# Where plain up parts end and block products begin: a four-layer hybrid trunk with one more plain part, later adaLN steps and another eviction

## The chip, the cores and the metric

The kernel runs on 1 core of a Trainium2 chip. The metric is device time in microseconds (us) of one execution; the median of several runs counts. The engines are TensorE (PE in the profile; PEld is its weight load), VectorE (DVE), ScalarE (ACT), GpSimd (POOL) and SyncE (SP, which only issues transfers here).

## The reference

The reference is two residual layers on x of shape (1024 tokens, 1024 channels) in float32, conditioned by a vector c. Each layer has a mixer and a channel mixer (FFN):

```python
for i in range(DEPTH):                         # DEPTH = 2
    mod = (silu(c) @ ada_w[i] + ada_b[i])      # adaLN: 6 x 1024 numbers
    sh_m, sc_m, g_m, sh_f, sc_f, g_f = split(mod, 6)
    hm = rms_norm(x, norm_mix[i]) * (1 + sc_m) + sh_m
    x = x + g_m * (even_mixer(hm) if i % 2 == 0 else odd_mixer(hm))
    hf = rms_norm(x, norm_ffn[i]) * (1 + sc_f) + sh_f
    x = x + g_f * conv_ffn(hf)

def conv_ffn(h, w_up, conv_w, conv_b, w_down):  # w_up 1024 x 5632, w_down 2816 x 1024
    gate, val = split(h @ w_up, 2)
    gate = causal_dwconv(gate, conv_w) + conv_b # width 3
    return (silu(gate) * val) @ w_down
```

The even mixer is gated linear attention in parallel with trailing-window pooling. The odd mixer is attention in three groups of 8 heads (dilations 1, 4 and 16 of the window); the groups' outputs are merged per head with weights from their softmax denominators, and an output projection of 1024 x 1024 follows:

```python
wts = softmax(stack(lses), axis=0)
o = sum(wts[..., None] * stack(outs), axis=0)
return o.reshape(B, T, 1024) @ w_out
```

## The kernel before, in words

Channels lie on the 128 partitions and tokens along the free dimension: x is 8 tiles of 128 x 1024, and every stage handles the tokens in two halves of 512 columns. Each float32 operand of a large product is split into a rounded high part and the rest (`split`, L185 on ACT and L186 on POOL or DVE), and one product of 128 x 128 by 128 x 512 becomes three matmuls: high x high, high x low, low x high (`mm3`, L212 to L214; L1392 to L1394 in the attention projections).

The kernel is written with a framework that plans the order on every engine when it is built: instructions that come earlier in the source have priority, and one whose inputs or buffers are not free yet, by the planner's own estimates of durations, is passed over for a later one. The order so planned is fixed. At run time each engine works through its own list and waits where an operand or a buffer is not there. `tc.issue_after(ins)` puts what is issued in its block behind `ins` on its engine.

The source's own order is made by generators. `weave(chain, dense)` runs a latency-bound chain of steps and, at each number that the chain yields, takes as much of a dense generator (one step is three matmuls) as that number of microseconds; `None` from the dense side means that it has nothing to give.

PSUM has two tiles of two banks (`mm_ps`, names `mm`) and four of one bank (`s_ps`, names `sp`). Buffers in SBUF that matter here: 24 of 128 x 1024 (`big`), 4 of raw weights (`raw`), 9 pairs of split weights (`whi`, `wlo`), 8 of 128 x 512 (`t2k`).

**The FFN's up projection** (`ffn`). It has 22 tiles (j), each of a gate and a value output of 128 channels. `first_two` computes tiles 0 and 1 directly: eight row blocks for each output and half, 96 `mm3` matmuls a tile. It starts on token half 0 while half 1 is still being normalised, and its last chain is the value output of tile 1, half 1, in an `mm_ps` tile that `act` (L1167) reads. The other tiles are formed from block products (`up`): 2 x 2 blocks of the weights and of h, seven products of 12 matmuls in place of eight, and sums before and after them. `h_sums` forms the sums of h once a layer (L1210, in place on the normalised x, then splits into `ext`, `t4` and the second half of h's own tiles), `w_sums(j)` those of the weights (L1265, four DVE additions, loads `wr` or, for the first such tile, `raw`), and `plus` (L1282) those of the products, which also frees their PSUM. In the source `w_sums(j + 1)` stands before `up(j)`. `conv` and `act` finish a tile (L1146, L1142, L1165, L1167) and store it to DRAM (`hid`).

The call of these steps before:

```python
sums = first_two()
a = w_sums(2)
if l == 0:
    secs_due[0], pace[0] = 24, 9
    with tc.issue_after(last_act[0].ins):
        step_back(True)
        step_back(True)
b = sums()
for j in range(2, NJ):
    nxt = w_sums(j + 1) if j < NJ - 1 else None
```

**adaLN.** The 24 sections of modulation columns are summed in the background. `step_back` is called with every group of three matmuls of the FFN and, once in `pace` calls, takes one step of `ada_steps`: a load of 256 KB into `raw` (L274, on SP) and one multiply-add, on DVE (L288, L290) while `by_pool` is false, on ACT and POOL (L284, L286) in the down projection, where `pace` is 2. A section takes ten steps; at the first FFN 14 sections are left.

**Attention** (`odd`). `dense` runs 12 projections of queries and keys and 6 of values; each qk part ends with a norm on ACT and DVE (L1403 to L1410) and, ten dense steps later, with the transposes on PE (L1424). `chains` runs 12 attention parts (`attend`), each of 24 steps. `merge(hp, need)` loads the three groups' outputs of one head pair (`ld`, three buffers, L1624, on SP), forms the weights on DVE and ACT (L1626 to L1634), sums (L1639 on ACT, L1641 on DVE) and transposes (L1647); it has eight load steps that yield `need` and four transposing ones that yield half of it. Two merges stand in the source after the attention parts 5 and 6, two more at the end, where `dense` has come to the output projection.

**The output projection** adds gate x (w_out rows x merged heads) to x, two row blocks at a time for head pairs 0 and 1 (`update` with `wide`), then four for pairs 2 and 3. With `wide="apart"` each 128 x 512 half of an `mm_ps` tile is scaled by ACT (L250) into a `t2k` tile and added by POOL (L251). With `wide=True`, which the even layer uses, one DVE instruction of 128 x 1024 (L253) does both when both halves are there.

Of the kernel before, what the change touches and what calls it, by code (L numbers as in the profile page):

```python
# [13 lines left out]
ALU = mybir.AluOpType  # L14
# [20 lines left out]
def trunk(ctx, tc, x, c, ada_w, ada_b, norm_mix, norm_ffn, ev_w_in, ev_w_out, gdn_conv_w,  # L35
# [35 lines left out]
    def t2k():  # L71
        return tmp("t2k", [P, HALF], 8)
# [153 lines left out]
    def update(rows, hid, gate, xt, order, wide=False, done=None):  # L226
# [7 lines left out]
        for o, hf in order:  # L234
# [10 lines left out]
            if not wide:  # L245
                nc.vector.scalar_tensor_tensor(out=xt[o][:, s], in0=p, scalar=gate[:, o:o + 1], in1=xt[o][:, s],  # L246
                                               op0=ALU.mult, op1=ALU.add)
            elif wide == "apart":
                t = t2k()
                nc.scalar.activation(t, p, AF.Copy, scale=gate[:, o:o + 1])  # L250
                nc.gpsimd.tensor_tensor(out=xt[o][:, s], in0=xt[o][:, s], in1=t, op=ALU.add)  # L251
            elif hf:
                nc.vector.scalar_tensor_tensor(out=xt[o], in0=ps, scalar=gate[:, o:o + 1], in1=xt[o],  # L253
                                               op0=ALU.mult, op1=ALU.add)
# [876 lines left out]
    def ffn(l, xt, h, vec, acc, vec_next):  # L1131
        gate = mod[l][:, 40:48]
        wu, wd = ffn_w_up[l], ffn_w_down[l]
        with tc.tile_pool(name=f"pf{l}", bufs=1) as pf:
# [25 lines left out]

            last_act = [None]

            def act(t, vps, j):

                nc.scalar.activation(t, t, AF.Silu)  # L1165
                for hf in range(2):
                    last_act[0] = nc.vector.tensor_tensor(out=t[:, HS[hf]], in0=t[:, HS[hf]], in1=vps[hf], op=ALU.mult)  # L1167
                nc.sync.dma_start(hid_d[l][j], t)
# [34 lines left out]
            KH = KT // 2  # L1203

            def h_sums():

# [30 lines left out]
            def w_sums(j):  # L1237

                raw = []
                for c0 in (j * P, DFF + j * P):  # L1240
                    if j == 2:
                        for q in range(2):
# [27 lines left out]
            def up(j, b, a):  # L1270
# [24 lines left out]
                act(t, (u, v), j)  # L1295

            sums = first_two()
            a = w_sums(2)
            if l == 0:
                secs_due[0], pace[0] = 24, 9  # L1300
                with tc.issue_after(last_act[0].ins):
                    step_back(True)
                    step_back(True)
            b = sums()
            for j in range(2, NJ):
                nxt = w_sums(j + 1) if j < NJ - 1 else None
# [21 lines left out]
    def odd(xt, h, vec, acc):  # L1328
# [5 lines left out]
        with tc.tile_pool(name="po", bufs=1) as po:  # L1334
# [130 lines left out]
            def dense():  # L1465
# [43 lines left out]
                for ks in ((0, 1), (2, 3)):  # L1509
                    upd = update(row_blocks(od_w_out[0], ks), o, gate, res["x"], BY_TILE, wide="apart")  # L1510
                    for n, c in enumerate(upd):
# [158 lines left out]
            def chains():  # L1670
                last = len(todo) - 1
                for i in range(last):
                    yield lambda: (i, 0) in ready
                    yield from attend(i, 1.7)
                    if i in (5, 6):
                        yield from merge(i - 5, 2.0)
                other = merge(2, 0)
# [91 lines left out]
```

## Time and profile before

| | |
|---|---|
| median of 3 runs | 3075.42 us (3072.78 to 3076.55) |
| the profiled execution | 3068.5 us, span 3066.5 us |
| PE busy | 2961.2 us, 97% of the span, 14362 matmuls |
| DVE busy | 1946.5 us, 63% |
| ACT, POOL busy | 1148.7 us (37%), 1056.6 us (34%) |
| granted PE clock, mean | 0.989 |
| DMA | 331.46 MB, 108 GB/s over the span |

A busy PE is an overlapped pipeline: a matmul of 512 columns is shown as about 0.39 us but the next starts 0.226 us later, so counts and start times tell more than busy shares. A line of the timeline has start, duration (both us), engine, source line, operation, what it writes and reads, how many alike were joined, and in brackets the idle time before it with what ended it. The stages of the span: the even mixer to about 545 us, the first FFN to about 1245, attention to about 2390, the second FFN to the end.

### The profile page before, as it was taken

The numbers are of one execution on the slowest core, as the hardware profiler recorded it, in microseconds if no ns is written. First come the engines' busy times: TensorE is split into PE (matmuls) and PEld (weight loads), VectorE is DVE, ScalarE is ACT, GpSimd is POOL, SyncE is SP. The second block draws the span as 40 slices with busy tenths as digits, with TensorE's granted clock in tenths as the row PEclk, the third lists the DMA queues.
The fourth block names the chain that finished last, engine by engine and source line by source line (L and its number), as shares of the span: only waits on it lengthen the run. The fifth ranks groups of instructions, "written<-read, shape, count | busy, mean of one in ns | idle before, by whom it ended". The sixth has DMA issues, their size and how long they took to land.

```text
span 3066.5 us, 40355 instructions
## 1 busy us (share of the span) xinstructions
PE 2961.2 (97%) x14362; PEld 2439.3 (80%) x14362; DVE 1946.5 (63%) x3770; ACT 1148.7 (37%) x2285; POOL 1056.6 (34%) x807
## 2 busy tenths in 40 slices
PE   7999999999999999999999999999988899999999
PEld 4777777778888888788888878888866688888888
DVE  6768735998886555554545546463667877766554
ACT  5434422533334433434243323333354433334210
POOL 3322223555556865200000000000064555556540
PEclk9999999999999999999999999999999999999999
DMA  7313323253333654413233242322243222224321
GB/s 257 107 46 99 89 80 133 76 182 113 110 118 133 211 156 139 145 35 102 62 95 89 80 127 77 108 71 94 72 169 106 81 84 83 83 83 168 110 91 58
DMA packets 274754, 331.46 MB, mean 108 GB/s; under 512 B 27155, under 2 KB 194170, under 8 KB 274554
## 3 DMA queue, kind: packets, MB, share of 16 engines
q1 hardware_dynamic: 266554, 300.54, 31.2%
q0 software_dynamic: 7040, 25.17, 2.4%
q10 hardware_dynamic: 960, 3.18, 0.3%
q8 instruction: 113, 1.85, 0.2%
q14 instruction: 87, 0.71, 0.1%
HBM read 251.82 MB, written 77.00 MB: 107 GB/s over the span
## 4 chain that ended last, share of the span: by engine, by line
PE 67%; DVE 8%; POOL 3%; DMA 3%; issue 3%; ACT 1%; SPq 0%; POOLq 0%; ACTq 0%; DVEq 0%
PE sp L212 9%; PE sp L214 9%; PE sp L213 9%; PE mm L1394 8%; PE mm L1392 8%; PE mm L1393 8%; PE mm L212 3%; PE mm L213 3%; PE mm L214 3%; PE sp L1588 2%; PE sp L1544 2%; PE sp L1424 1%; POOL ada_acc L286 1%; POOL wlo L186 1%; DVE t2k L1641 1%
## 5 line engine op out<-in xcount | busy, mean ns | idle before, releaser
L1392 PE MATMUL mm<-whi,hh 128*128 128x512 f32 x1152 | 483.0, 419 | 0.0
L1394 PE MATMUL mm<-whi,hl 128*128 128x512 f32 x1152 | 452.9, 393 | 0.0
L1393 PE MATMUL mm<-wlo,hh 128*128 128x512 f32 x1152 | 450.9, 391 | 0.0
L186 POOL TENSOR_TENSOR wlo<-raw,whi 128x512 fp32r<-128x512 f32 x190 | 249.8, 1329 | 477.8 <-ACT whi L185 431.2
L246 DVE SCALAR_TENSOR_TENSOR xr<-sp,mod,xr 128x512 f32<-128x512 f32 x336 | 251.4, 750 | 180.4 <-PE sp L214 179.6
L185 ACT ACTIVATE whi<-raw 128x512 fp32r<-128x512 f32 x334 | 208.2, 629 | 299.9 <-PE sp L213 103.8
L212 PE MATMUL sp<-oh,whi 128*128 128x512 f32 (+1 forms) x832 | 312.7, 376 | 0.0
L214 PE MATMUL sp<-oh,wlo 128*128 128x512 f32 (+1 forms) x832 | 310.4, 373 | 0.8 <-POOL wlo L186 0.8
L213 PE MATMUL sp<-ol,whi 128*128 128x512 f32 (+1 forms) x832 | 310.2, 373 | 0.0
L212 PE MATMUL mm<-hh,whi 128*128 128x512 f32 x720 | 290.5, 405 | 7.5 <-DVE hh L400 3.0
L213 PE MATMUL mm<-hl,whi 128*128 128x512 f32 x720 | 284.9, 396 | 7.7 <-DVE hl L401 6.4
L214 PE MATMUL mm<-hh,wlo 128*128 128x512 f32 x720 | 284.4, 395 | 0.0
L186 POOL TENSOR_TENSOR wlo<-t2k,whi 128x512 fp32r<-128x512 f32 x160 | 229.9, 1452 | 149.7 <-ACT whi L185 109.7
L1489 POOL DMA_DIRECT2D vd<-v x24 | 17.6, 735 | 762.5 <-ACT v L1486 388.1
L1394 PEld LDWEIGHTS mm<-whi,hl 128*128 128x128 f32 x1152 | 216.3, 188 | 48.2
L1393 PEld LDWEIGHTS mm<-wlo,hh 128*128 128x128 f32 x1152 | 217.8, 189 | 37.2
L1392 PEld LDWEIGHTS mm<-whi,hh 128*128 128x128 f32 x1152 | 217.4, 189 | 35.9
L186 POOL TENSOR_TENSOR wlo<-wr,whi 128x512 fp32r<-128x512 f32 x114 | 178.0, 1564 | 163.5 <-ACT whi L185 157.4
L214 PEld LDWEIGHTS sp<-oh,wlo 128*128 128x128 f32 x832 | 156.7, 188 | 28.8 <-POOL wlo L186 1.2
L213 PEld LDWEIGHTS sp<-ol,whi 128*128 128x128 f32 x832 | 156.8, 189 | 27.0
L212 PEld LDWEIGHTS sp<-oh,whi 128*128 128x128 f32 x832 | 156.8, 188 | 27.1 <-ACT whi L185 0.3
L213 PEld LDWEIGHTS mm<-hl,whi 128*128 128x128 f32 x720 | 136.2, 189 | 38.0 <-DVE hl L401 9.2
(395 smaller groups left out, 6254.2 us busy)
## 6 DMA issues: line engine op xcount, KB each, us to landing
raw<-in_ada_w_dram SPq DMA_DIRECT2D x160, 256.0 KB
wr<-in_ffn_w_up_dram SPq DMA_DIRECT2D x76, 512.0 KB
raw<-in_od_w_in_dram SPq DMA_DIRECT2D x144, 256.0 KB
hid<-ft SPq DMA_DIRECT2D x44, 512.0 KB
raw<-in_ffn_w_down_dram SPq DMA_DIRECT2D x88, 256.0 KB
big<-hid SPq DMA_DIRECT2D x44, 512.0 KB
xr<-xs SPq DMA_DIRECT2D x32, 512.0 KB
os<-stg SPq DMA_DIRECT2D x96, 130.0 KB
```

The costliest lines, as they stand in the source:

```text
L185: nc.scalar.activation(dst_hi, src, AF.Copy)
L186: eng.tensor_tensor(out=dst_lo, in0=src, in1=dst_hi, op=ALU.subtract)
L212: nc.tensor.matmul(ps, wh, mh, start=first, stop=False)
L213: nc.tensor.matmul(ps, wh, ml, start=False, stop=False)
L214: return nc.tensor.matmul(ps, wl, mh, start=False, stop=last)
L246: nc.vector.scalar_tensor_tensor(out=xt[o][:, s], in0=p, scalar=gate[:, o:o + 1], in1=xt[o][:, s], op0=ALU.mult, op1=ALU.add)
L286: nc.gpsimd.tensor_tensor(out=acc, in0=acc, in1=raw, op=ALU.add)
L1392: nc.tensor.matmul(p, hh, wh, start=(k == 0), stop=False)
L1393: nc.tensor.matmul(p, hh, wl, start=False, stop=False)
L1394: nc.tensor.matmul(p, hl, wh, start=False, stop=(k == KT - 1))
L1544: nc.tensor.matmul(ps[:, at:at + len(ks) * P], qks[i][0][:, hh, blk * P:(blk + 1) * P], qks[i][1][:, hh, ks[0] * P:(blk + 1) * P], start=T ...
L1588: nc.tensor.matmul(ps[:, j * P:(j + 1) * P], pTs[n][:, a0 + c * P:a0 + (c + 1) * P], vb(kb, hh), start=(c == 0), stop=(c == len(ks) - 1))
```

## The change

Five edits. (1) Tile 2 of the up projection in both layers is computed directly by the new function `third`, in the order gate and value for half 1, gate for half 0, convolution, value for half 0; the block products begin with tile 3 (`J0`). `third` stands before `w_sums(J0)`, whose weights now come in four pieces through `raw`. (2) The adaLN steps in the first FFN no longer begin with two forced steps behind the second tile, at one in nine, but at tile 4, at one in seven. (3) The attention output projection for head pairs 0 and 1 uses `wide=True` in place of `wide="apart"`, which is removed. (4) The merges after attention parts 5 and 6 yield 3.5 and 1.75 in place of 2.0 and 1.0. (5) `last_act` is gone.

```diff
--- before.py
+++ after.py
@@ -245,10 +245,6 @@
             if not wide:
                 nc.vector.scalar_tensor_tensor(out=xt[o][:, s], in0=p, scalar=gate[:, o:o + 1], in1=xt[o][:, s],
                                                op0=ALU.mult, op1=ALU.add)
-            elif wide == "apart":
-                t = t2k()
-                nc.scalar.activation(t, p, AF.Copy, scale=gate[:, o:o + 1])
-                nc.gpsimd.tensor_tensor(out=xt[o][:, s], in0=xt[o][:, s], in1=t, op=ALU.add)
             elif hf:
                 nc.vector.scalar_tensor_tensor(out=xt[o], in0=ps, scalar=gate[:, o:o + 1], in1=xt[o],
                                                op0=ALU.mult, op1=ALU.add)
@@ -1158,13 +1154,11 @@
                 if hf:
                     taps(t, g[0], j, lambda i: (HALF, HALF + i), lambda i: (HALF - i, HALF))
 
-            last_act = [None]
-
             def act(t, vps, j):
 
                 nc.scalar.activation(t, t, AF.Silu)
                 for hf in range(2):
-                    last_act[0] = nc.vector.tensor_tensor(out=t[:, HS[hf]], in0=t[:, HS[hf]], in1=vps[hf], op=ALU.mult)
+                    nc.vector.tensor_tensor(out=t[:, HS[hf]], in0=t[:, HS[hf]], in1=vps[hf], op=ALU.mult)
                 nc.sync.dma_start(hid_d[l][j], t)
 
             def gate_tile(name="ft", dt=F32):
@@ -1202,6 +1196,19 @@
 
             KH = KT // 2
 
+            J0 = 3
+
+            def third(j):
+
+                gp, vp = mm_ps(), mm_ps()
+                wb = units_c(wu, (j * P, DFF + j * P))
+                t = gate_tile()
+                drain(units([gp, vp], wb, h, (1,)))
+                drain(units([gp], wb[:1], h, (0,)))
+                conv(t, gp, j)
+                drain(units([vp], wb[1:], h, (0,)))
+                act(t, [vp[:, s] for s in HS], j)
+
             def h_sums():
 
                 for k in range(KH):
@@ -1238,7 +1245,7 @@
 
                 raw = []
                 for c0 in (j * P, DFF + j * P):
-                    if j == 2:
+                    if j == J0:
                         for q in range(2):
                             raw.append(raw_tile())
                             nc.sync.dma_start(raw[-1].rearrange("p (k c) -> p k c", k=KH),
@@ -1294,15 +1301,14 @@
                 conv(t, g, j)
                 act(t, (u, v), j)
 
+            secs_due[0] = 0
             sums = first_two()
-            a = w_sums(2)
-            if l == 0:
-                secs_due[0], pace[0] = 24, 9
-                with tc.issue_after(last_act[0].ins):
-                    step_back(True)
-                    step_back(True)
+            third(2)
+            a = w_sums(J0)
             b = sums()
-            for j in range(2, NJ):
+            for j in range(J0, NJ):
+                if l == 0 and j == J0 + 1:
+                    secs_due[0], pace[0] = 24, 7
                 nxt = w_sums(j + 1) if j < NJ - 1 else None
                 if nxt is None:
                     hid = [from_dram(hid_d[l][i]) for i in (0, 1)]
@@ -1507,7 +1513,7 @@
                     res["x"] = reload(xs[1])
                 o = [[granule(osp2[i][:, s]) for s in HS] for i in range(2)]
                 for ks in ((0, 1), (2, 3)):
-                    upd = update(row_blocks(od_w_out[0], ks), o, gate, res["x"], BY_TILE, wide="apart")
+                    upd = update(row_blocks(od_w_out[0], ks), o, gate, res["x"], BY_TILE, wide=True)
                     for n, c in enumerate(upd):
                         if turn:
                             run_turn(1)
@@ -1673,7 +1679,7 @@
                     yield lambda: (i, 0) in ready
                     yield from attend(i, 1.7)
                     if i in (5, 6):
-                        yield from merge(i - 5, 2.0)
+                        yield from merge(i - 5, 3.5)
                 other = merge(2, 0)
                 for n, need in enumerate(attend(last, 1.3)):
                     yield need
```

## The prediction

> **What bounds the kernel now.** I read the page first: busy times, then the chain that ended last.
>
> ```profile
> PE 2961.2 (97%) x14362; PEld 2439.3 (80%) x14362; DVE 1946.5 (63%) x3770; ACT 1148.7 (37%) x2285; POOL 1056.6 (34%) x807
> PE 67%; DVE 8%; POOL 3%; DMA 3%; issue 3%; ACT 1%; SPq 0%; POOLq 0%; ACTq 0%; DVEq 0%
> ```
>
> The profiled execution took 3068.5 us (span 3066.5); the median of the runs is 3075.4, 6.9 more. TensorE (PE) carries the chain. Next the windows by stage: engines with busy us and instructions, then the granted clock.
>
> ```profile
> 640.00:697.21 57.21, 57.21 (x256) 47.39 (x255) 53.38 (x63) 19.84 (x30) 30.30 (x20) 1.00 0.50 155
> 2235.00:2345.00 110.00, 89.24 (x400) 69.05 (x399) 72.62 (x178) 56.49 (x136) 64.69 (x49) 0.91 0.44 148
> ```
>
> While the first FFN forms block products (first row), PE has no idle time: 57.21 us, 256 matmuls; only their number counts. In the tail of attention 400 instructions take 110 us: waits count. The timeline (start, us, engine, line, idle before and its releaser) names the waits. First where the block products start, layer 0, PE and then VectorE (DVE):
>
> ```profile
> 594.81 0.47 PE L212 MATMUL mm<-hh,whi 128*128 128x512 f32 x1
> 603.06 0.39 PE L212 MATMUL sp<-hh,whi 128*128 128x512 f32 x1
> 616.43 0.39 PE L214 MATMUL sp<-hh,wlo 128*128 128x512 f32 x1
> 622.58 0.79 PE L212 MATMUL sp<-t,whi 128*128 128x512 f32 x1 [5.76 <-DVE ft L1282]
> 623.17 0.63 PE L213 MATMUL sp<-t,whi 128*128 128x512 f32 x1
> 623.60 0.63 PE L214 MATMUL sp<-t,wlo 128*128 128x512 f32 x1
> ...
> 627.01 0.57 PE L213 MATMUL sp<-t,whi 128*128 128x512 f32 x1
> ...
> 562.39 0.69 DVE L1265 TENSOR_TENSOR t2k<-raw,raw 128x512 f32<-128x512 f32 x1 [2.57 <-DMA raw<-in_ffn_w_up_dram]
> 603.78 3.17 DVE L186 TENSOR_TENSOR hl<-xr,hh 128x512 fp32r<-128x512 f32 x2
> 607.47 0.67 DVE L1167 TENSOR_TENSOR ft<-ft,mm 128x512 f32<-128x512 f32 x1
> 616.61 0.77 DVE L1265 TENSOR_TENSOR t2k<-wr 128x512 f32<-128x512 f32 x1 [1.29 <-DMA wr<-in_ffn_w_up_dram]
> 621.85 0.67 DVE L1282 TENSOR_TENSOR ft<-t2k,sp 128x512 f32<-128x512 f32 x1
> ```
>
> Five products of 12 matmuls lie between 603.06 and 616.43, 0.226 us a matmul. The last plain chain starts at 594.81 and has 24, so it ends at 600.3; six block products run to 616.7. The seventh needs a PSUM buffer that the first sum (L1282, 621.85) frees. That sum stands behind the next tile's weight sums (L1265), which waited for a load until 616.61. Layer 1, PE then DVE:
>
> ```profile
> 2431.36 0.39 PE L214 MATMUL sp<-ext,wlo 128*128 128x512 f32 x1
> 2433.63 0.50 PE L212 MATMUL mm<-hh,whi 128*128 128x512 f32 x1 [1.88 <-DVE ft L1167]
> 2441.72 0.39 PE L214 MATMUL sp<-hh,wlo 128*128 128x512 f32 x1
> 2446.81 0.80 PE L212 MATMUL sp<-t,whi 128*128 128x512 f32 x1 [4.70 <-DVE ft L1282]
> 2447.41 0.63 PE L213 MATMUL sp<-t,whi 128*128 128x512 f32 x1
> ...
> 2432.90 0.68 DVE L1167 TENSOR_TENSOR ft<-ft,mm 128x512 f32<-128x512 f32 x1
> 2440.76 0.84 DVE L1265 TENSOR_TENSOR t2k<-wr 128x512 f32<-128x512 f32 x1 [4.61 <-DMA wr<-in_ffn_w_up_dram]
> ```
>
> The same, and one stall more: the fourth product waits for the two-bank PSUM buffer that the second plain tile's gating (L1167) frees. Then attention: PE's three long waits and the 4.06, then DVE, SyncE (SP) and GpSimd (POOL) beside them:
>
> ```profile
> 1808.14 2.35 PE L1424 MATMUL sp<-ident,t2k 128*128 128x128 f32 x8 [5.24 <-DVE t2k L1410]
> 2248.60 0.66 PE L1424 MATMUL sp<-ident,t2k 128*128 128x128 f32 x2 [7.03 <-DVE t2k L1410]
> 2274.72 0.80 PE L212 MATMUL mm<-whi,whi 128*128 128x512 f32 x1 [4.06 <-ACT t2k L250]
> 2308.59 0.45 PE L1647 MATMUL sp<-ident,t2k 128*128 128x128 f32 x1 [5.40 <-DVE t2k L1641]
> ...
> 1803.38 0.16 DVE L1626 TENSOR_REDUCE mx<-ld 128x2 f32<-128x6 f32 x1 [7.58 <-DMA ld<-os]
> 2262.43 6.46 DVE L1641 SCALAR_TENSOR_TENSOR t2k<-ld,me,t2k 128x128 f32<-128x128 f32 x4
> 2301.34 8.41 DVE L1641 SCALAR_TENSOR_TENSOR t2k<-ld,me,t2k 128x128 f32<-128x128 f32 x8 [7.22 <-ACT t2k L1639]
> ...
> 1793.63 4.68 SPq L1624 DMA_DIRECT2D ld<-os  x6
> ...
> 2296.58 7.52 POOL L251 TENSOR_TENSOR xr<-xr,t2k 128x512 f32<-128x512 f32 x6
> ```
>
> **Part 1: the stalls that a third plain tile covers.** It puts 96 matmuls, 21.7 us, between 600.3 and the first block product. The first sum could run at 605.8 (two products) and ran at 621.85, 16 us late; the tile gives more. What is late next: the splits into h's second half now wait for the tile's reads of it, some 11 us, and the load behind them; 616.61 becomes 628, while the seventh product comes at 638. Gain in layer 0: 622.58 - 616.43 - 0.23 = 5.9 us, and ten matmuls (to 627.01) at 0.43 us in place of 0.226, 2.2: 8.1. Layer 1: 2.0 + 4.9, and 1.6 at the slow rate: 8.5. Sum -16.6.
>
> **Part 2: its own matmuls.** A plain tile has 2 outputs x 8 rows x 2 halves x 3 = 96, a block tile 7 x 4 x 3 = 84. 12 x 2 layers x 0.226 = +5.4, fully on the path. Four weight loads stand on SP's queue in place of the block tile's four; the next tile's come as four pieces instead of two, of the same bytes, behind weight buffers that the first two tiles free as they end: 0.
>
> **Part 3: a new wait.** There are two two-bank PSUM buffers. The second plain tile's value half holds one until L1167 ends (608.15; 2433.58 in layer 1). Today the fourth product wants it, 8.2 us after the plain tiles; `third` wants it at once, for its value output, which alternates with its gate. Lower bound: the planner lets the gate's 48 matmuls (10.8 us) go first: 0. Upper bound: the source's order, three gate matmuls first: 608.15 - 601.0 = 7.1, and 2433.58 - 2424.1 = 9.5 (layer 1's plain tiles end 36 matmuls before 2431.6, at 2423.4). I take a point between. The planner reorders (L1265 ran at 562.39, ahead of a norm that the source has before it) but by ordinary durations: the two splits at 603.78 took 3.17 us in place of 2 x 0.68, and by that plan DVE is some 4 us late. In the plan, then, the buffer is free about 604, after four or five gate steps (12 to 15 matmuls, 603.0 to 603.7). That leaves stalls of 4 and 6 us; after stalls of 4.06 and 4.70 above PE went slow, after the 1.88 not: 1 and 2 us more. Sum +13; ends 0 and 20. Part 1 of the Trainium skill's page TensorE: Matmul & The Clock Gate says that an idle window of about 3.4 us halves the clock until a busy one; 0.43 against 0.226 agrees. By that rule both stalls pay about 1.7, 0.4 more than I take.
>
> FFN together: -16.6 + 5.4 + 13 = +1.8. The third tile buys nothing.
>
> **Part 4: adaLN steps.** Groups by line (count, busy us, mean ns):
>
> ```profile
> L290 DVE SCALAR_TENSOR_TENSOR ada_acc<-raw,cs,ada_acc 128x512 f32<-128x512 f32 x85 | 88.0, 1035 | 11.6 <-DMA raw<-in_ada_w_dram 10.7
> L286 POOL TENSOR_TENSOR ada_acc<-ada_acc,raw 128x512 f32<-128x512 f32 x55 | 71.8, 1306 | 22.5 <-ACT ada_acc L284 12.8 <-ACT raw L284 6.9 <-DVE ada_acc L290 0.6
> ```
>
> Two forced steps and 20 x 28 / 9 = 62 become 18 x 28 / 7 = 72: 0.9 more a tile on DVE, 1.04 us each, 2.8 us in a window of 57.21. With 53.38 busy in layer 0's window DVE reaches 56.2, under PE's 57.2: 0. Should it become the bound there, up to +3. Their loads on SP now follow the weight loads of tiles 3 and 4 instead of preceding them, which frees those. Eight fewer steps on POOL and ScalarE (ACT) fall in the down projection, beside a busy PE: 0.
>
> **Part 5: merges spread (2.0 to 3.5).** A merge spans 60 steps of dense work rather than 40. DVE stood 7.58 us on a merge load (1803.38, issued from 1793.63 on), behind it the norm that PE's transposes wanted: 5.24 us, then a slow stretch, about 8 in all. Three load buffers lead by three merge steps, of four, then six dense steps of three matmuls (0.68 us): 8.2 us, then 12.2, against the 10 that this load took. I take -6; ends -8 and +5 (the merge now runs beside two norms, and the attention part after the second merge ends four steps later).
>
> **Part 6: output projection evicted by DVE.** 32 ACT and 32 POOL instructions go, 16 on DVE of 1024 columns come, as in the even layer (L253 and its waiters):
>
> ```profile
> L250 ACT ACTIVATE t2k<-mm,mod 128x512 f32<-128x512 f32 x32 | 21.5, 684 | 19.3 <-PE mm L214 19.2
> L251 POOL TENSOR_TENSOR xr<-xr,t2k 128x512 f32<-128x512 f32 x32 | 41.4, 1319 | 17.4 <-ACT t2k L250 9.4 <-DMA ld<-os 4.1 <-issue 3.9
> L253 DVE SCALAR_TENSOR_TENSOR xr<-mm,mod,xr 128x1024 f32<-128x1024 f32 x16 | 20.5, 1282 | 16.3 <-PE mm L214 16.3
>   PE mm L212: 0.4, 1
> L1641 DVE SCALAR_TENSOR_TENSOR t2k<-ld,me,t2k x128: 333/345/6571, 1735.4 to 2338.7; 128x128 f32<-128x128 f32 x128
> ```
>
> POOL's adds lie on DVE: while six ran without a gap (2296.58 to 2304.1), eight L1641 took 8.41 us, one of them 6.57; its median is 0.345. PE's 5.40 us at 2308.59 are for these; the 4.06 at 2274.72 are for ACT's eviction. With the slow stretches 7.5 + 6, and 1.5 in smaller waits: -15. GPSIMD Engine Reference (8. Key points) of the Trainium skill has POOL share its SBUF interfaces with VectorE, in contention where DVE has two SBUF inputs; L1641 has two, the new eviction one, so by that rule the whole 15 goes with the adds. Against it 16 x 1.28 = 20.5 us more on DVE, which is busy 72.6 of 110, 10.7 of them stretched. Lower end 0.4, what the same form cost PE in the even layer; upper end all 20.5. Here two chains share DVE in order, but a buffer has 2.7 us (12 matmuls) of grace, so I take +5, nearer the even row. Net -10; ends -15 and +5. The 7.03 at 2248.60 wait for a norm behind merge work, and stay.
>
> **Sum.** +1.8 - 6 - 10 = -14, against 3068.5 as against the median; with a little for the smaller norm waits -15: 3060.
>
> **The rivals.** (a) The planner puts the gate first, and the value buffer is no wait: 13 less than the sum, 3047. For it: it reorders. Against: DVE's 4 us of delay are unplanned, and nothing passes a matmul that waits: PE stood 1.88 us for L1167. MATMULs stay in program order, by the Trainium skill (TensorE: Matmul & The Clock Gate, Step-by-step); the trace agrees. (b) Attention's stalls are replaced: its norms come late for their own reasons, as at 2248.60, and parts 5 and 6 give nothing: +2, 3077. (c) Slower: DVE becomes the evictor that PE waits for, each of the 16 behind chain work that itself waits for ACT or a load. From 1 us each beyond the grace part 6's 15 are gone; at 1.28 + 0.7 each it is +32 - 15, with +2 and -6: +13, 3088. For it: DVE's waits of 7.58 and 7.22 us above; against it: the 0.4.
>
> **How the numbers follow.** Chances: forecast 0.42, (a) 0.22, (b) 0.20, (c) 0.12, else 0.04. About 0.2%, 6.2 us, is what a measurement of this kernel tells from no change. The forecast, (a) and a little of the rest are faster, 0.66; (b) is the same, 0.20; (c) and a little slower, 0.14. The range holds the forecast, (b) and most of (a): 3043 to 3079; the forecast's own is 3052 to 3068.
>
> **What would show it.** Part 1: no PE wait over 1 us for L1282 where block products start. Part 3: in `third`, PE's first value matmul waits for L1167, 4 and 6 us; none is (a). Part 4: L290 near 91, L286 near 49, no idle PE in layer 0. Part 5: no wait over 4 us of L1626 for a load. Part 6: no L250 or L251, L1641 never over 2 us, PE waits for L253 of some 5 us. The forecast fails if these pass 15 us, or if the loads and splits that `third` covers come late again.

## Result and the profile after

The changed kernel takes 3056.4 us (median of 5 runs, 3050.1 to 3061.4) against 3075.4: 0.9937 of the time before, 95% interval 0.992 to 0.9953, 19.0 us faster. 3060 had been forecast. The profiled execution took 3055.1 us (span 3053.3), 13.4 less than that of before. The end is near the forecast, but three of its terms are not: two were too favourable and one not favourable enough. One of e6's five executions below, the profiled one, ran at a granted clock of 0.847 and took 3297.7 us, so e6 goes by the median of its other four and has no stage lengths.

The page of the changed kernel, busy times and the chain that ended last:

```profile
PE 2965.5 (97%) x14386; PEld 2449.4 (80%) x14386; DVE 1938.5 (63%) x3770; ACT 1125.9 (37%) x2239; POOL 996.0 (33%) x763
PE 77%; DVE 5%; issue 1%; DMA 1%; ACT 1%; POOL 0%; SPq 0%; DVEq 0%; POOLq 0%; ACTq 0%
```

PE has 24 matmuls more, as counted, and its share of the chain rose from 67% to 77%.

Where the time went is read by stages, between four rows of PE's timeline that both kernels have: the first matmul of the first FFN into a one-bank buffer, the first attention projection, the first matmul behind the second FFN's last norm row, and the last output transposes. Before, then after:

```profile
551.55 0.39 PE L212 MATMUL sp<-hh,whi 128*128 128x512 f32 x1
1238.14 0.39 PE L1392 MATMUL mm<-whi,hh 128*128 128x512 f32 x1
2392.03 0.47 PE L212 MATMUL sp<-hh,whi 128*128 128x512 f32 x1
3061.42 0.60 PE L1702 MATMUL sp<-ident,xr 128*128 128x128 f32 x4
```

```profile
555.23 0.39 PE L212 MATMUL sp<-hh,whi 128*128 128x512 f32 x1
1246.11 0.39 PE L1398 MATMUL mm<-whi,hh 128*128 128x512 f32 x1
2377.55 0.48 PE L212 MATMUL sp<-hh,whi 128*128 128x512 f32 x1
3047.58 0.60 PE L1708 MATMUL sp<-ident,xr 128*128 128x128 f32 x4
```

First FFN 686.6 before and 690.9 after (+4.3), attention 1153.9 and 1131.4 (-22.5), second FFN 669.4 and 670.0 (+0.6; the table below counts it from the last norm row to the last output transpose and has 669.7 and 670.4). What lies before 551.55 is touched by no edit, and PE, VectorE and ACT run it in the same order in both kernels. It ended at 551.2 to 557.2 us in thirteen profiles of this study, so its 3.7 us more in the profile after are scatter. The stages without it change by -17.5.

The windows whose rows of before the prediction shows, after:

```profile
640.00:697.21 57.21, 57.21 (x254) 47.33 (x253) 41.15 (x47) 19.91 (x29) 30.29 (x21) 1.00 0.33 107
2235.00:2345.00 110.00, 102.03 (x494) 83.77 (x495) 89.15 (x229) 45.57 (x120) 28.32 (x20) 0.97 0.50 164
```

In the block products PE is as full as before. In the tail of attention it does 494 instructions, not 400, in the same 110 us, at a granted clock of 0.97, not 0.91; VectorE is busier (89.15 us for 72.62) and POOL idler (28.32 for 64.69). The two windows do not hold quite the same work, since attention starts 8 us later after the change (1246.11 for 1238.14).

The two FFNs first. PE's timeline after, layer 0 and layer 1 (start, us, engine, line; in brackets the idle time before, and its releaser). L1161 is the gating that was L1167, L1138 the convolution that was L1142:

```profile
608.41 0.80 PE L212 MATMUL mm<-hh,whi 128*128 128x512 f32 x1 [3.62 <-DVE ft L1161]
609.01 0.63 PE L213 MATMUL mm<-hl,whi 128*128 128x512 f32 x1
...
635.14 0.77 PE L212 MATMUL mm<-hh,whi 128*128 128x512 f32 x1 [5.38 <-DVE ft L1138]
...
2415.18 0.80 PE L212 MATMUL mm<-hh,whi 128*128 128x512 f32 x1 [3.62 <-DVE ft L1161]
...
2416.20 0.63 PE L214 MATMUL mm<-hh,wlo 128*128 128x512 f32 x1
```

The waits for the sums (L1282 before) are gone. The wait for the value buffer, 3.62 us, is in both layers. Layer 0 has a second one, 5.38 us, for the third tile's convolution, which frees the gate's buffer. VectorE before it:

```profile
600.05 0.69 DVE L186 TENSOR_TENSOR ext<-xr,ext 128x512 fp32r<-128x512 f32 x1
...
615.19 1.51 DVE L284 TENSOR_SCALAR ada_acc<-raw,cs 128x512 f32<-128x512 f32 x1
616.63 1.78 DVE L186 TENSOR_TENSOR t<-xr,t 128x512 fp32r<-128x512 f32 x1
618.33 1.77 DVE L286 SCALAR_TENSOR_TENSOR ada_acc<-raw,cs,ada_acc 128x512 f32<-128x512 f32 x1
...
621.72 2.44 DVE L286 SCALAR_TENSOR_TENSOR ada_acc<-raw,cs,ada_acc 128x512 f32<-128x512 f32 x2
...
629.53 2.42 DVE L286 SCALAR_TENSOR_TENSOR ada_acc<-raw,cs,ada_acc 128x512 f32<-128x512 f32 x2
631.88 1.27 DVE L1138 SCALAR_TENSOR_TENSOR ft<-mm,cols,ft 128x1023 f32<-128x1023 f32 x1
```

The adaLN steps (L284, L286) that the source starts at tile 4 run from 615.19 on, in the middle of the third tile: the planner put them there. Six stand ahead of the convolution's first instruction (631.88), 8.1 us of work (e12's expectation below counts eight), between splits (L186) that take 1.78 us where one at 600.05 took 0.69. On SP their first four loads were issued ahead of tile 4's weights, `wr`:

```profile
609.63 7.43 SPq L270 DMA_DIRECT2D raw<-in_ada_w_dram  x4
618.43 4.54 SPq L1255 DMA_DIRECT2D wr<-in_ffn_w_up_dram  x4
```

Attention after, PE and then SP and VectorE:

```profile
1813.69 2.35 PE L1430 MATMUL sp<-ident,t2k 128*128 128x128 f32 x8 [3.99 <-DVE t2k L1416]
...
2249.05 0.38 PE L1583 MATMUL sp<-ident,sb 128*128 128x128 f32 x2
2253.72 0.80 PE L212 MATMUL mm<-whi,whi 128*128 128x512 f32 x1 [4.29 <-DVE xr L249]
...
2259.69 1.04 PE L1430 MATMUL sp<-ident,t2k 128*128 128x128 f32 x8
...
2296.77 1.16 PE L1594 MATMUL sp<-v,sb 128*128 128x128 f32 x8 [2.98 <-DVE sb L1585]
2298.02 0.63 PE L213 MATMUL mm<-ol,whi 128*128 128x512 f32 x1
```

```profile
1797.80 2.99 SPq L1630 DMA_DIRECT2D ld<-os  x6
```

```profile
1796.56 2.22 DVE L1647 SCALAR_TENSOR_TENSOR t2k<-ld,me,t2k 128x128 f32<-128x128 f32 x8 [3.13 <-ACT t2k L1645]
1805.23 0.17 DVE L1632 TENSOR_REDUCE mx<-ld 128x2 f32<-128x6 f32 x1 [5.28 <-DMA ld<-os]
```

Of the four waits of before one is left, 3.99 us at 1813.69: the norm that it is for stands on VectorE behind two waits for merge loads, 5.28 us (1805.23) and 2.45 us more at 1809.14. At 2249 PE no longer waits 7.03 us for the norm: its transposes (L1430, 2259.69) now stand behind 18 projection matmuls, the first of which waits 4.29 us for the new eviction (L249). The two later waits (4.06, 5.40) went, 2.98 came. From the first projection to the transposes ahead of that place (2249.05; before, the row below) both kernels take 1003 us (1002.9, 1002.8): all that attention gained lies behind it:

```profile
2240.97 0.60 PE L1577 MATMUL sp<-ident,sb 128*128 128x128 f32 x4
```

### The profile page after: what moved, and what is told of

Same layout as the page of the kernel before. It is cut to its first block, busy times and chain, and to the rows that moved or that the text cites. A ratio compares the mean times of both kernels' runs of the same rounds, so it can differ in the third digit from the quotient of the medians.

```text
span 3053.3 us, 40242 instructions
## 1 busy us (share of the span) xinstructions
PE 2965.5 (97%) x14386; PEld 2449.4 (80%) x14386; DVE 1938.5 (63%) x3770; ACT 1125.9 (37%) x2239; POOL 996.0 (33%) x763
## 4 chain that ended last, share of the span: by engine, by line
PE 77%; DVE 5%; issue 1%; DMA 1%; ACT 1%; POOL 0%; SPq 0%; DVEq 0%; POOLq 0%; ACTq 0%
PE sp L214 12%; PE sp L212 12%; PE sp L213 12%; PE mm L1400 8%; PE mm L1398 8%; PE mm L1399 8%; PE mm L212 3%; PE mm L213 3%; PE mm L214 3%; PE sp L1594 2%; PE sp L1550 2%; PE sp L1430 1%; PE sp L1583 1%; DVE xr L1217 1%; DVE t2k L1647 0%
## 5 line engine op out<-in xcount | busy, mean ns | idle before, releaser
L186 POOL TENSOR_TENSOR wlo<-raw,whi 128x512 fp32r<-128x512 f32 x198 | 261.9, 1336 | 517.8 <-ACT whi L185 464.3
L212 PE MATMUL mm<-hh,whi 128*128 128x512 f32 x768 | 312.2, 408 | 18.3 <-DVE ft L1161 7.2
L213 PE MATMUL mm<-hl,whi 128*128 128x512 f32 x768 | 306.5, 399 | 6.7 <-DVE hl L397 6.0
L214 PE MATMUL mm<-hh,wlo 128*128 128x512 f32 x768 | 306.0, 399 | 0.0
L186 POOL TENSOR_TENSOR wlo<-t2k,whi 128x512 fp32r<-128x512 f32 x152 | 215.4, 1429 | 163.1 <-ACT whi L185 107.2
L186 POOL TENSOR_TENSOR wlo<-wr,whi 128x512 fp32r<-128x512 f32 x108 | 168.1, 1557 | 164.3 <-ACT whi L185 157.3
L212 PEld LDWEIGHTS mm<-hh,whi 128*128 128x128 f32 x768 | 147.3, 192 | 50.2 <-issue 11.6
```

The source lines that it names most:

```text
L186: eng.tensor_tensor(out=dst_lo, in0=src, in1=dst_hi, op=ALU.subtract)
L212: nc.tensor.matmul(ps, wh, mh, start=first, stop=False)
L213: nc.tensor.matmul(ps, wh, ml, start=False, stop=False)
L214: return nc.tensor.matmul(ps, wl, mh, start=False, stop=last)
```

## The experiments

Lengths of the stages in us from each kernel's profile, and medians of 4 to 12 runs (before on the same chips: 3074.9 to 3078.5). "Third" is the tile computed directly, "wide" the eviction by VectorE.

| kernel | first FFN | attention | second FFN | median | ratio to before (95%) |
|---|---|---|---|---|---|
| before | 686.6 | 1153.9 | 669.7 | 3075.4 | |
| after | 690.9 | 1131.4 | 670.4 | 3056.4 | 0.9937 (0.9920 to 0.9953) |
| e1: third alone | 705.1 | 1151.1 | 670.7 | 3086.5 | 1.0040 (1.0026 to 1.0055) |
| e10: third, one in seven | 690.8 | 1152.6 | 670.2 | 3074.4 | 0.9997 (0.9988 to 1.0006) |
| e2: after without third | 687.5 | 1137.4 | 671.2 | 3056.8 | 0.9940 (0.9925 to 0.9954) |
| e3: after, apart | 691.0 | 1152.3 | 670.3 | 3073.8 | 0.9993 (0.9984 to 1.0002) |
| e4: after, merges at 2.0 | 690.6 | 1134.5 | 670.6 | 3055.5 | 0.9939 (0.9925 to 0.9953) |
| e8: after, ACT then VectorE | 690.8 | 1141.2 | 670.7 | 3060.9 | 0.9951 (0.9935 to 0.9967) |
| e9: after, POOL adds beside | 690.1 | 1144.5 | 670.5 | 3068.2 | 0.9977 (0.9965 to 0.9989) |
| e5: after, value in one-bank buffers | 680.3 | 1132.4 | 663.7 | 3039.6 | 0.9881 (0.9863 to 0.9899) |
| e6: after, gate first | - | - | - | 3036.7 | 0.9868 (0.9849 to 0.9886) |
| e7: after, adaLN from tile 6 | 691.1 | 1134.3 | 670.4 | 3057.2 | 0.9945 (0.9931 to 0.9958) |
| e12: after, adaLN held back | 684.3 | 1132.7 | 670.1 | 3051.1 | 0.9909 (0.9892 to 0.9927) |
| e11: e5, e7's edit, merges at 5.0 | 682.6 | 1126.6 | 663.7 | 3032.9 | 0.9866 (0.9852 to 0.9879) |

A stage whose source is unchanged repeats: first FFN 690.1 to 691.0 in five profiles, second FFN with the third tile as in the change 670.1 to 670.7 in nine. Attention with the change's source took 1131.4, 1132.4, 1132.7, 1134.3 and 1137.4, so there a difference under 6 us tells nothing.

**e1, the third tile alone.** The function `third` and `J0 = 3` as in the change; the forced adaLN steps behind `act2`, the pace of nine, the merges and the eviction as before.

```diff
             sums = first_two()
+            act2 = last_act[0]
+            third(2)
-            a = w_sums(2)
+            a = w_sums(J0)
             ...                                  # the forced steps: behind act2
```

> The kernel before with the third plain tile alone; adaLN steps (two forced ones behind the second tile, then one in nine), merges and eviction as before. Lengths of stages in the two profiles so far: first FFN (its first matmul into a one-bank buffer to the first attention projection) 686.6 us before, 690.9 after; attention (to the last norm's transposes of the second FFN) 1153.9 and 1131.4; second FFN (from there to the last output transpose) 669.7 and 670.4. Theory 1, the third tile buys nothing, since a wait for its value buffer (3.8 us in both layers, plus a slow stretch) and 12 more matmuls take what the covered stalls give, and in layer 0 the adaLN steps cost a second wait: first FFN 689 to 693, second 670.4, attention as before at 1154; in all +3 to +6 us, 3078 to 3081. Theory 2, the second wait of layer 0 (5.5 us, for the gating convolution L1138) comes from where the change puts the adaLN steps: here it is gone or moved and the first FFN is 683 to 686; in all about -2. Theory 3, attention gained through what the FFN before it leaves behind: attention 1131 to 1145 here too.

Measured: 3086.5, and a first FFN 18.5 us longer than before, more than any theory allowed. Both waits of the third tile are there, and a new one comes in the down projection, for POOL's adaLN sum. PE's timeline:

```profile
1204.98 1.11 PE L328 MATMUL sp<-ident,ada_acc 128*128 128x128 f32 x4 [3.82 <-POOL ada_acc L286]
```

Groups of e1 by line (count, busy us, mean ns):

```profile
L286 POOL TENSOR_TENSOR ada_acc<-ada_acc,raw 128x512 f32<-128x512 f32 x56 | 72.8, 1301 | 31.8 <-ACT raw L284 19.9 <-ACT ada_acc L284 10.0
```

One tile of block products fewer means fewer of the steps that VectorE takes. 56 are left for POOL (55 before, 49 after), the last section is late, and PE waits 3.82 us and then goes on slowly (from 1200 to 1260 it does 223 instructions at a granted clock of 0.89). Theory 3 fell: attention stayed at 1151.

**e10, the same with the pace at one in seven.**

```diff
-                secs_due[0], pace[0] = 24, 9
+                secs_due[0], pace[0] = 24, 7
```

> The kernel before with the third tile, as in the first experiment, its two forced adaLN steps kept, but the rest at one in seven, not one in nine. There the first FFN took 705.1 us, 14.2 more than in the changed kernel, with a 4.0 us wait of PE for POOL's last adaLN sum near 1201 and slow matmuls behind it. Theory 1 (one tile less in which steps are taken leaves the last section late, and only the pace matters): that wait is gone, first FFN 690 to 692, in all 3071 to 3074. Theory 2 (the early start is what costs): first FFN 700 to 705, 3083 to 3087.

Measured: first FFN 690.8, in all 3074.4. Theory 1: with 44 additions left for POOL in place of 56 the wait is gone. The pace alone is worth 14.3 us once the third tile is there, and the early start costs nothing more than the change's.

**e2, the change without the third tile.** Edit: `J0 = 2`, no `third(2)`.

> The changed kernel without the third tile: block products from tile 2 on, adaLN steps from tile 3 on at one in seven. Theory 1 (the third tile buys nothing): PE's waits for L1282's line where block products start are back (5.9 us in layer 0, 2.0 and 4.9 in layer 1), the second FFN is 669.7 as before, the first 684 to 690, attention 1131; in all 3051 to 3056, no slower than the changed kernel. Theory 2 (the later adaLN steps are worth something by themselves): the first FFN is under 683, below that of both kernels. Rival (the third tile is what pays): both FFNs longer than in the changed kernel, by 5 us or more in sum, 3061 or more.

The stalls came back. PE's timeline, layer 0 and layer 1 (L1289 is the sum):

```profile
627.55 0.79 PE L212 MATMUL sp<-t,whi 128*128 128x512 f32 x1 [5.64 <-DVE ft L1289]
...
2420.09 0.50 PE L212 MATMUL mm<-hh,whi 128*128 128x512 f32 x1 [1.89 <-DVE ft L1161]
2433.34 0.79 PE L212 MATMUL sp<-t,whi 128*128 128x512 f32 x1 [4.79 <-DVE ft L1289]
```

But the two FFNs are 1358.7 in sum, against 1361.3 with the third tile: the tile costs 2.6 us and pays nothing. In all 3056.8, as the changed kernel. Theory 1 holds; theory 2 falls (687.5, not under 683).

**e3, the eviction apart again; e4, the merges at 2.0 again.**

```diff
-  upd = update(..., BY_TILE, wide=True)       # e3, with the branch for "apart" put back
+  upd = update(..., BY_TILE, wide="apart")
-                        yield from merge(i - 5, 3.5)      # e4
+                        yield from merge(i - 5, 2.0)
```

> The changed kernel with the eviction of head pairs 0 and 1 apart on ACT and POOL again; merges stay spread at 3.5. Attention stage. Theory 1 (the prediction's split, eviction 10 of the 16 and merges 6, scaled to the 22.5 measured): attention 1143 to 1147, L1641's copies up to 6 us again beside POOL's adds, in all 3068 to 3072. Rival 1 (the eviction gave all of it): 1152 to 1154, 3077. Rival 2 (the spread merges gave all): 1131 to 1134, 3057.

> The changed kernel with the two merges at 2.0 again; the eviction stays on DVE. Theory 1 (the prediction's split): attention 1137 to 1142, PE's wait for the norm behind the merge's load back at 5 us or more near 1808, in all 3062 to 3067. Rival 1 (merges give nothing, the changed kernel still waits 4.2 us there): 1130 to 1133, 3057. Rival 2 (the spread costs something at the end, where the attention parts come later): under 1130, 3052.

e3: attention 1152.3, rival 1: the eviction gave all of it. The waits of before are back on PE, and one copy of L1651 (L1641 before) is stretched again; the same line in the changed kernel:

```profile
2254.67 0.66 PE L1434 MATMUL sp<-ident,t2k 128*128 128x128 f32 x2 [7.06 <-DVE t2k L1420]
2281.12 0.79 PE L212 MATMUL mm<-whi,whi 128*128 128x512 f32 x1 [4.06 <-ACT t2k L250]
2315.15 0.45 PE L1657 MATMUL sp<-ident,t2k 128*128 128x128 f32 x1 [5.29 <-DVE t2k L1651]
```

```profile
L1651 DVE SCALAR_TENSOR_TENSOR t2k<-ld,me,t2k x128: 336/346/6462, 1742.1 to 2345.4; 128x128 f32<-128x128 f32 x128
```

```profile
L1647 DVE SCALAR_TENSOR_TENSOR t2k<-ld,me,t2k x128: 332/347/2293, 1743.1 to 2313.2; 128x128 f32<-128x128 f32 x128
```

e4: 1134.5 and 3055.5, nothing to tell from the changed kernel. PE's wait behind the merge loads is 4.74 us there, 3.99 in the changed kernel. The spread to 3.5 gave nothing that can be measured.

**e8, ACT scales and VectorE adds; e9, POOL adds beside the new eviction.** They are to split the eviction's 20.9 us (1152.3 - 1131.4).

```diff
+            elif wide == "apart":                                             # e8
+                t = t2k()
+                nc.scalar.activation(t, p, AF.Copy, scale=gate[:, o:o + 1])
+                nc.vector.tensor_tensor(out=xt[o][:, s], in0=xt[o][:, s], in1=t, op=ALU.add)
+                if wide == "beside":                                          # e9, after the eviction
+                    for q in range(2):
+                        t = t2k()
+                        nc.gpsimd.tensor_tensor(out=t, in0=xt[o][:, HS[q]], in1=xt[o][:, HS[q]], op=ALU.add)
```

> The changed kernel with the output projection of head pairs 0 and 1 scaled out of PSUM by ACT, half by half as before, and added by VectorE (not POOL). The output is the same. Attention is 1152.3 with ACT and POOL and 1131.4 with VectorE alone. Theory 1 (the gain is POOL's adds leaving VectorE alone): 1130 to 1137, no copy of L1647's line over 2.5 us. Theory 2 (the gain is that ACT no longer evicts, the 4.3 us wait for it and a late free PSUM buffer): 1145 to 1152. In all 3055 to 3062 or 3070 to 3077.

> The changed kernel with 32 additions of 128 x 512 put on POOL again beside the merges, after each eviction by VectorE, into tiles that nothing reads; PE waits for none of them. Theory 1 (contention of POOL's adds with VectorE): L1647's copies reach 4 us and more beside them and attention rises from 1131.4 to 1140 to 1152. Theory 2 (only the eviction's own engine counts): 1130 to 1135, within 3 us of the changed kernel.

e8's attention lies between the theories, 1141.2: by that 11.1 of the 20.9 come with the adds leaving POOL and 9.8 with ACT leaving the eviction. Its profiled execution was the longest of six, though. By the medians, e3 3073.8, e8 3060.9 and the changed kernel 3056.4, the parts are 12.9 and 4.5, and 3060.9 lies in theory 1's range; the intervals of the last two overlap. So POOL's adds are the larger part, and whether ACT's leaving is worth 4 or 10 us stays open. With POOL's adds the long copy goes (longest 1.43 us), and with it PE's 5.29. The 7.06 stays:

```profile
2256.62 0.66 PE L1434 MATMUL sp<-ident,t2k 128*128 128x128 f32 x2 [7.06 <-DVE t2k L1420]
...
2281.38 0.50 PE L212 MATMUL mm<-whi,whi 128*128 128x512 f32 x1 [1.80 <-ACT t2k L250]
```

```profile
L1651 DVE SCALAR_TENSOR_TENSOR t2k<-ld,me,t2k x128: 338/346/1426, 1744.0 to 2336.7; 128x128 f32<-128x128 f32 x128
```

e9 costs 13.0 us of attention, inside theory 1's range, but not by its sign: no copy reaches 4 us (the longest took 2.08), though L1651 is busy longer in sum than in the changed kernel. Groups by line, of e9 and then of the changed kernel:

```profile
L1651 DVE SCALAR_TENSOR_TENSOR t2k<-ld,me,t2k 128x128 f32<-128x128 f32 x128 | 50.2, 450 | 11.9 <-ACT t2k L1649 11.7
```

```profile
L1647 DVE SCALAR_TENSOR_TENSOR t2k<-ld,me,t2k 128x128 f32<-128x128 f32 x128 | 43.8, 398 | 11.8 <-ACT t2k L1645 11.5
```

That is 6.4 us more on VectorE. The added tiles also hold buffers and the planner's order differs, so how much of the 13 is contention is not shown.

**e5, the third tile's value in one-bank buffers; e6, its gate first.**

```diff
-                gp, vp = mm_ps(), mm_ps()                                     # e5
+                gp, v = mm_ps(), [s_ps(), s_ps()]
-                drain(units([gp, vp], wb, h, (1,)))
+                drain(units([gp, v], wb, h, (1,)))
                 ...                              # its later drain and act take v for vp
-                drain(units([gp, vp], wb, h, (1,)))                           # e6
-                drain(units([gp], wb[:1], h, (0,)))
+                drain(units([gp], wb[:1], h, (1, 0), half_outer=True))
                 conv(t, gp, j)
-                drain(units([vp], wb[1:], h, (0,)))
+                drain(units([vp], wb[1:], h, (1, 0), half_outer=True))
```

> The changed kernel with the third tile's value output in two one-bank PSUM buffers instead of the two-bank one that tile 1's gating (L1161 there) frees; nothing else. Theory 1 (the prediction's part 3: the 3.75 us wait at the third tile's first value matmul is for that buffer, and costs 3.75 plus some 2 to 3 us of slow matmuls): the wait is gone in both layers; second FFN 670.4 -> 664 to 666. In the first FFN it goes too, 690.9 -> 684 to 686, and the 5.5 us wait for the convolution stays. Rival 1: in the first FFN VectorE is the bound there, so that the next wait grows by what the first loses: first FFN 689 to 692, second 664 to 666. Rival 2: the wait is for VectorE whatever buffer is asked for: both FFNs within 1 us of the changed kernel. In all 3045 to 3050 by theory 1.

> The changed kernel with the third tile's 48 gate matmuls (both halves) before its 48 value matmuls; the buffers as in the change. Theory 1 (the value buffer is the wait, and 10.8 us of gate matmuls cover it; rival (a) of the prediction forced by hand): no wait of PE for the gating line in the third tile; second FFN 664 to 666, first FFN 684 to 686 or, if the convolution, which now comes earlier, no longer stands behind the adaLN steps, 677 to 681. Rival: h's second half is read 48 matmuls longer, so the splits into it come late and the block products wait: FFNs as in the changed kernel or longer.

e5: the wait is gone in both layers. The second FFN is 663.7, 6.7 us shorter, a little better than theory 1. The first is 680.3, 10.6 shorter, where theory 1 had 684 to 686 with the wait for the convolution as it was. Of that wait only this is left on PE:

```profile
634.71 0.47 PE L212 MATMUL mm<-hh,whi 128*128 128x512 f32 x1 [2.06 <-DVE ft L1138]
```

In all 3039.6, below theory 1's 3045. e6 gives 3036.7, 19.7 below the changed kernel, where theory 1 had 9 to 20 by its stages: the buffer was the wait, and either way around it works. That the splits into h's second half come too late, the rival, is not borne out by the time.

**e7, adaLN from tile 6; e12, adaLN held back.** Is the wait for the convolution due to the adaLN steps?

```diff
-                if l == 0 and j == J0 + 1:                                    # e7
-                    secs_due[0], pace[0] = 24, 7
+                if l == 0 and j == J0 + 3:
+                    secs_due[0], pace[0] = 24, 6
+                elif k == 0 and hold[0]:          # e12: hold[0] is the third tile's last gating, layer 0
+                    with tc.issue_after(hold[0].ins):
+                        nc.vector.tensor_scalar(out=acc, in0=raw, scalar1=cs[:, 0:1], ...)
```

> The changed kernel with the adaLN steps starting two tiles later (tile 6 in place of tile 4) at one in six (74 steps in place of 72); the third tile's buffers as in the change. It tells whether the 5.5 us wait of layer 0 for the third tile's convolution, which layer 1 does not have, is due to the adaLN steps that stand between on VectorE (12 of them between 615 and 636 us). Theory 1 (it is): the wait is gone or under 1 us, first FFN 690.9 -> 682 to 685, in all about 3049. Theory 2 (VectorE is late there with sums and splits alone): first FFN 688 to 692, 3055 to 3058.

> The changed kernel with each section's first adaLN instruction on VectorE held behind the third tile's last gating (in the order of VectorE's list), so that none of the eight adaLN instructions that ran between 615 and 632 us stands ahead of the third tile's convolution; the start at tile 4 and the one in seven stay. The run with the start moved to tile 6 could not tell this, since VectorE's list came out the same there. Theory 1 (these steps make the convolution late): 8.1 us of them go from ahead of it, the 5.5 us wait is gone or under 1 us, first FFN 690.9 -> 682 to 685, second FFN 670.4 and attention 1131 to 1137 as before, in all 3047 to 3052. Theory 2 (sums and splits alone, which take 1.75 us in place of 0.69 there, make it late): a wait of 3 us or more stays, first FFN 687 to 692, 3054 to 3058.

e7 could not tell: 691.1. Its first adaLN step still runs inside the third tile:

```profile
614.32 1.51 DVE L284 TENSOR_SCALAR ada_acc<-raw,cs 128x512 f32<-128x512 f32 x1
```

e12 tells: 684.3, the wait shrunk to 0.55 us, and 3051.1 in all. VectorE and PE:

```profile
625.73 0.69 DVE L1278 TENSOR_TENSOR t2k<-wr 128x512 f32<-128x512 f32 x1 [5.10 <-DMA wr<-in_ffn_w_up_dram]
```

```profile
632.11 0.47 PE L213 MATMUL mm<-hh,whi 128*128 128x512 f32 x1 [0.55 <-DVE ft L1142]
```

Theory 1 holds: the steps made the convolution late, and cost 6.6 us. VectorE now reaches the convolution (629.37) behind weight sums that waited 5.10 us for their load (625.73).

**e11, a version to beat both.** e5, the adaLN steps as in e7, and `merge(i - 5, 5.0)`.

> A version meant to beat both kernels: the change, with the third tile's value in one-bank buffers (first FFN 680.3, attention 1132.4, second FFN 663.7 when that was done alone), the adaLN steps from tile 6 on at one in six, and the first two merges at 5.0 in place of 3.5. Theory 1 (a merge still waits for its load, 4.1 us near 1800, and more dense work between its steps covers that; the 2.2 us left in the first FFN go with the adaLN steps): first FFN 677 to 679, attention 1127 to 1130, second FFN 663.7, in all 3031 to 3036. Rival (spreading has no more to give, since it ends only with the loads' buffers; or the attention parts after it come later): attention 1131 to 1138, in all 3036 to 3042.

3032.9, the lowest median here, 42 us below the kernel before. At 5.0 no matmul of PE is late by more than 0.5 us between 1700 and 2000, and attention is 1126.6, 5.8 under e5's; of the seven profiles with the new eviction and nothing else changed in attention but the merges, it is the only one below 1131, though by one profile. The first FFN came out at 682.6, not 677 to 679: moving the start in the source moves nothing on VectorE (e7). e6, 3036.7, is not clearly apart from it.

## Why the prediction was right in sum, point by point

**Part 1, right.** No wait for the sums is left where the block products start, and e2 brings back 5.64, 1.89 and 4.79 us where before had 5.76, 1.88 and 4.70.

**Part 2, right.** 14386 matmuls against 14362.

**Part 3, right in sum; both of its sizes were off.** The wait is where it was said to be, 3.62 us in each layer, where 4 and 6 were taken. The prediction's own working, 12 to 15 matmuls ahead of the wait, gives more than it took: 4.4 to 5.1 in layer 0 and 6.8 to 7.5 in layer 1. From start to start each stall costs 3.8, and the slow matmuls behind it 1.7 us in layer 0 and 2.8 in layer 1, where 1 and 2 were taken: 12.1 in sum, 13 taken. With the wait gone, layer 1 gains 6.7 us (e5). The rule of the Trainium skill (TensorE: Matmul & The Clock Gate, Part 1), that an idle window of about 3.4 us halves the clock until a busy one, agrees: 3.62 us idle brought 0.43 us a matmul in both layers (609.01, 2416.20), 2.06 us in e5 did not. The estimate of 1.7 for each that the prediction makes from it is what layer 0 paid; layer 1's stretch was longer.

**Part 4, wrong.** It was put at 0, and two things hid in it. The step that failed first is that the loads "now follow the weight loads of tiles 3 and 4": the steps of tile 4 went into the third tile (615.19), with their loads (609.63) ahead of tile 4's weights (618.43), made its convolution late, and cost 6.6 us (e12). The second is "Eight fewer steps on POOL and ScalarE (ACT) fall in the down projection, beside a busy PE: 0". Fewer is harmless, but with the third tile and the old pace there are 56 in place of e10's 44, and that costs 14.3 us (e1 against e10): the 0 was right only because the pace changes too. Where between 44 and 56 the cost begins was not tried. VectorE's busy time in the window of the block products, forecast to rise to 56.2 us, fell to 41.15. The counts themselves came out as forecast:

```profile
L286 DVE SCALAR_TENSOR_TENSOR ada_acc<-raw,cs,ada_acc 128x512 f32<-128x512 f32 x91 | 90.4, 993 | 13.2 <-DMA raw<-in_ada_w_dram 12.1
L282 POOL TENSOR_TENSOR ada_acc<-ada_acc,raw 128x512 f32<-128x512 f32 x49 | 63.7, 1300 | 17.8 <-ACT raw L280 8.2 <-ACT ada_acc L280 7.9
```

91 and 49.

**FFN in sum.** +1.8 was forecast, +4.9 measured. Layer 1 is +0.7, and its terms give 2.7 + 6.6 - 8.5 = +0.8. Layer 0 is +4.3; its terms with the convolution's 6.6 give 2.7 + 5.5 + 6.6 - 8.1 = +6.7. The other 2.4 are about what two waits of before make up that the forecast did not count and that are not there after, 1.59 us for a norm at 568.05 and 0.78 us for a split weight at 1195.59.

**Part 5, wrong.** -6 was taken, nothing is seen (e4, and the 1003 us of both kernels up to the output projection). The step that failed is the lead: loads were to run three merge steps ahead, 12.2 us at the new spread against 10 for the load. The load of 1797.80 is issued when its buffer comes free, with the eight sums of 1796.56, and these had waited 3.13 us for ACT. VectorE wants the load right behind them, and stands 5.28 us, until 1805.23: the lead was some 2 us, not 12.2. Only at 5.0 does PE's wait go (e11).

**Part 6, right in kind, half its size.** -10 was taken; undoing it costs 17.4 us of the medians and 20.9 of the stage. By the stages POOL's adds were worth 11.1 and ACT's eviction 9.8, by the medians 12.9 and 4.5, where 7.5 and 6, and 1.5 for smaller waits, were taken ahead of the +5. The longest copy of the merge sums took 2.29 us after, where never over 2 was said. New waits for the eviction are 4.5 us (5 forecast), nearly all of it the 4.29. What was missed is that the 7.03 at 2248.60 would go: it stays in e3 and e8, with ACT evicting, and is gone with VectorE, where the planner puts the transposes later. Why it does was not tried. The half-speed matmuls behind the stalls went along (the clock of 0.97 for 0.91 above). On the Trainium skill's note (GPSIMD Engine Reference, 8. Key points): POOL's adds beside VectorE instructions with two SBUF inputs do stretch them (6.46 us in e3, 1.43 in e8 with the adds on VectorE). That they are the whole gain, which the prediction drew from it, does not fit e8's trace, where PE's 7.06 us stay, but e8's median does not exclude it.

**The sum.** Stages: +4.9 and -22.5 are -17.5; forecast +1.8, -6, -10 and -1. Part 4 and part 5 were too favourable, by 6.6 and 6, and part 6 not favourable enough, by 11; the 15 came near 17.5 because these offset each other, and that is luck. Rival (a), forced by hand in e6, is real and larger than its 13. Rival (b) did not come: the waits were replaced only in part (4.29 and 2.98 us for 7.03, 4.06 and 5.40). Rival (c) did not come: PE waits for the eviction at one place, not at 16.

## What to carry to other kernels

A planner's priority is not a position: work that "starts later" in the source need not run later. Here the first step ran at 615.19 us with its start at tile 4 and at 614.32 with its start at tile 6, in a bad place both times. So read its first start in the trace, and hold it behind an instruction if it must wait. Before a tile is added, ask which buffer its first matmul takes and who frees it: two one-bank buffers in place of one shared one were worth 17 us here, where the tile itself cost 2.6. And a background task's pace is sized by what is left at its deadline: 56 late additions in place of 44 cost 14 us.

## What was not expected of the hardware

Stretched VectorE instructions are short spells, not a steady tax: the same 128 x 512 split takes 0.69 us and 1.78 us within 17 us (600.05 and 616.63 in the changed kernel), and among 128 equal copies of e3 the median is 0.346 us and the longest 6.46. What the other engines did in each spell was not taken apart. And below the 3.4 us that the page of the Trainium skill named above has, the length of a wait alone did not tell whether PE slowed: 2.98 us at 2296.77 were enough (2298.02 shows 0.63 us), 2.06 in e5 were not. In e11, the first two rows here, 1.99 us were enough; in e12, the third, 3.03 us were not, and the matmuls behind it start 0.23 us apart. What decides was not tried.

```profile
631.38 0.47 PE L212 MATMUL mm<-hh,whi 128*128 128x512 f32 x1 [1.99 <-DVE ft L1138]
...
632.38 0.63 PE L213 MATMUL mm<-hl,whi 128*128 128x512 f32 x1
...
2294.92 1.16 PE L1600 MATMUL sp<-v,sb 128*128 128x128 f32 x8 [3.03 <-DVE sb L1591]
```
